# A two-layer diffusion trunk on one core: convolution gates by tanh, an earlier split of two gate slabs, lows on VectorE, and output projections in blocks of 512 columns

## The chip, the core and the metric

The kernel runs on one core of a Trainium2 chip. A core has a matrix engine (TensorE, in the profile PE, with its weight loads as PEld), a vector engine (VectorE, DVE), an engine for activation functions (ScalarE, ACT), a general engine (GpSimd, POOL) and SyncE (SP), whose queue starts all transfers that are spoken of here. Each engine works its instructions off in the order in which the program gave them; an instruction that has to wait holds up all behind it on its engine. SBUF is the memory on the chip, PSUM the banks that TensorE writes its products to, DRAM the memory beside it.

The metric is the time in microseconds (us) of one execution on the device. One execution is also recorded by the profiler; that record is the trace, and its summary is the page.

## The reference

Two layers, each with a token-mixing half and a channel half, on 512 latent tokens and 256 context tokens of width 1024, all in float32. The last layer gives the latent tokens alone, so that it needs only keys and values of the context. Cut to what matters here:

```python
hx = modulate(rmsnorm(x, norm1_g[i]), sx1, ax1)
px = hx @ w_in[i]          # conv input a, g | q | k | v | merge gates
z = a * jax.nn.sigmoid(g)                              # the convolution's gate
z = depthwise_conv(z, w_dw, width=31) + b_dw
y_conv = silu(layernorm(z)) @ w_conv_out
p = jax.nn.softmax(s, axis=-1)                         # 8 heads, two maps per head
w = p[:, :, 0] - lam * p[:, :, 1]
out = rmsnorm(w @ v, sub_g) * (1.0 - lam_init)
y_attn = out @ w_attn_out
g = jax.nn.sigmoid(gate_logits + b_gate)               # the merge gates, 2 x 1024 wide
x = x + gx1 * ((g_conv * y_conv + g_attn * y_attn) @ w_out)
x = x + gx2 * (square(relu(h2 @ w_mlp1)) @ w_mlp2)     # 4096 wide
```

The same runs on the context tokens with weights of the same name, in layer 0 whole, in layer 1 for keys and values.

## The kernel before, in words

**Products in three passes.** Every float32 operand x of a large product is split into a high part h (a copy in the matmul's own type, made on ScalarE) and a low part l = x - h (a subtraction). A product is three matmuls per contraction tile of 128, h by h, l by h and h by l (lines 142 to 144 in the trace). The splits are one helper; its high part is line 76 and its low part line 80, whichever tile they are for. Weights come in slabs of 1024 x 256, 1 MB each, into a staging tile (`r_...`), and are split there into `h_...` and `l_...`, each in two halves of 128x1024 elements. `load_slab` takes the engine of the lows: VectorE by default, GpSimd, or, with the pair `both`, one half on each.

**Stages of a layer.** (1) normalised input h1 in high and low, feature-major. (2) Attention, head by head: projections of q and k of the next head (`qk`, slabs `wqk`) and of v for the next pair of heads (`v`, slabs `wv`), scores `S`, exponentials `e` on ScalarE, the difference of the two maps on VectorE, transposes `wT` of the weights on TensorE, whose copies `wth`, `wtl` are made on ScalarE and VectorE, and the products `av`. (3) Convolution input `ca` and gate `cg`, two slabs each, four blocks of 128 features (`cg_0` to `cg_3`). (4) The merge gates `gt`, eight blocks for the attention branch (`gt_1_0` to `gt_1_7`, slabs `wg_1_0` to `wg_1_3`) and eight for the convolution (`gt_0_...`); meanwhile VectorE makes the convolution: 31 taps per block of channels, each tap one scalar_tensor_tensor into `crun` or, at the end, `cacc` (before: lines 1207 and 1211). (5) The branch projections `ya` and `yc`, the merged `mh`, `ml`. (6) The output projection `o` with residual and the sums of squares for the next norm. (7) The MLP (`f`, then `r`), in layer 0 by a scheme with fewer products, with a tail `r` that also ends in residual and sums of squares.

**What sets the order.** The function for a head is a generator; so are the projections and the conv blocks. `merge` draws from both in proportion to costs written in the code, head 7 with the conv blocks: `chain_(conv_a(0), conv_a(1), conv_g(0), conv_g1_ahead())`. A scheduler then orders each engine's instructions over the whole program, by its own estimates of when each can start; so an edit can move instructions far from the edited line. `issue_after` and `state["behind"]` name an instruction behind which others are put.

**Places that the change touches.** `conv_g`: four gate blocks go into PSUM tiles of two banks (`mm_tile`), ScalarE writes a sigmoid into a scratch tile with the tag `e0`, which the exponentials use too, and VectorE multiplies it into z. `conv_g1_ahead` takes one block of the second gate slab and then loads and splits the first merge-gate slab (1,0); slab (1,1) is split behind `ended`, the last head's final output copy. `spill_rstd`: the eight heads' reciprocal norms are transposed by TensorE (`rsT`), copied by VectorE (`rst`) and written to DRAM (`rs_d`). `branch_load` reads a head's output (`at_d` to `ar`) and, broadcast over the partitions, its reciprocal norm (`arb`), and VectorE multiplies them (before: line 1239). `out_slabs` makes the output projection (`o`) and the tail of the MLP (`r`); with a norm behind it, its first two slabs go by `halves`, that is column blocks of 256 tokens. `ada_beside` lays a count of small steps for the next layer's modulation beside each block.

## Time and profile before

| | |
|---|---|
| median of 3 runs | 2299.61 us (2297.89 to 2300.05) |
| profiled execution | 2294.07 us, span 2292.3 us |
| mean granted clock of TensorE | 0.995 |
| busy: PE, DVE, ACT, POOL | 97%, 73%, 46%, 29% |

The span is the time from the first to the last instruction; the rest of the execution's time lies around it. A row of waits reads: engine, its tile and line, "<-" the engine, tile and line that it waited for, then us in total, times, longest. A row in order of time reads: start, duration, engine, line, operation, tile written "<-" tiles read, shape; in brackets the idle time before it and what ended that. Matmuls are pipelined, so the distance of two starts, and not the duration, is what one costs.

Layer 0's conv gates lie at about 436 to 480 us of the span; layer 1's at about 1710 to 1742, its merge gates up to 1830, where `ya` begins.

### The profile page before, as it was taken

The numbers are of one execution on the slowest core, as the hardware profiler recorded it, in microseconds if no ns is written. First come the engines' busy times: TensorE is split into PE (matmuls) and PEld (weight loads), VectorE is DVE, ScalarE is ACT, GpSimd is POOL, SyncE is SP. The second block draws the span as 40 slices with busy tenths as digits, with TensorE's granted clock in tenths as the row PEclk, the third lists the DMA queues.
The fourth block names the chain that finished last, engine by engine and source line by source line (L and its number), as shares of the span: only waits on it lengthen the run. The fifth ranks groups of instructions, "written<-read, shape, count | busy, mean of one in ns | idle before, by whom it ended". The sixth has DMA issues, their size and how long they took to land.

```text
span 2292.3 us, 36448 instructions
## 1 busy us (share of the span) xinstructions
PE 2225.7 (97%) x14402; PEld 2015.7 (88%) x14402; DVE 1666.7 (73%) x2747; ACT 1053.5 (46%) x2049; POOL 655.3 (29%) x786
## 2 busy tenths in 40 slices
PE   7999999999999999999999998999999999999999
PEld 6999998888888999998999998999977889888887
DVE  6777776499657768787777567777758976757673
ACT  5555655422324264433445345565543333654542
POOL 1966775110000020222221347675722300100000
PEclk9999999999999999999999999999999999999999
DMA  9211111134444611332444522102114423443151
GB/s 318 60 34 44 47 46 47 45 116 160 138 150 147 212 46 57 98 119 88 132 139 142 167 75 58 45 24 63 45 61 130 131 93 120 147 129 100 66 184 37
DMA packets 202266, 232.62 MB, mean 101 GB/s; under 512 B 8864, under 2 KB 162928, under 8 KB 201968
## 3 DMA queue, kind: packets, MB, share of 16 engines
q1 hardware_dynamic: 202096, 230.30, 31.3%
q8 instruction: 113, 1.85, 0.3%
q14 instruction: 57, 0.47, 0.1%
HBM read 212.93 MB, written 17.35 MB: 100 GB/s over the span
## 4 chain that ended last, share of the span: by engine, by line
PE 73%; DVE 11%; ACT 5%; POOL 4%; DMA 4%; issue 2%; SPq 0%; DVEq 0%; POOLq 0%; ACTq 0%
PE r L151 4%; PE f L143 3%; PE f L144 3%; PE f L142 3%; PE r L143 3%; PE r L142 3%; PE r L144 3%; PE qk L142 2%; PE qk L143 2%; PE qk L144 2%; DVE crun L1211 2%; PE gt L142 2%; PE r L154 2%; PE gt L143 2%; PE gt L144 2%
## 5 line engine op out<-in xcount | busy, mean ns | idle before, releaser
L142 PE MATMUL qk<-h_wqk,h1h 128*128 128x256 f32 x640 | 182.6, 288 | 2.1 <-ACT rw L797 1.4
L143 PE MATMUL qk<-l_wqk,h1h 128*128 128x256 f32 x640 | 180.2, 284 | 0.0
L144 PE MATMUL qk<-h_wqk,h1l 128*128 128x256 f32 x640 | 176.4, 284 | 0.0
L969 DVE TENSOR_REDUCE st<-S 128x1 f32<-128x768 f32 (+1 forms) x160 | 134.5, 846 | 57.2 <-PE S L967 56.0
L972 ACT ACTIVATE e<-S,st 128x768 f32<-128x768 f32 (+1 forms) x160 | 131.0, 822 | 40.1 <-DVE st L969 39.8
L143 PE MATMUL f<-h2hl,h_w 128*128 128x512 f32 (+1 forms) x416 | 144.0, 348 | 1.1 <-POOL h2hl L80 0.9
L142 PE MATMUL f<-h2hh,h_w 128*128 128x512 f32 (+1 forms) x416 | 142.4, 348 | 2.1 <-ACT h2hh L387 1.1
L144 PE MATMUL f<-h2hh,l_w 128*128 128x512 f32 (+1 forms) x416 | 143.4, 346 | 0.0
L142 PE MATMUL gt<-h1h,h_wg 128*128 128x512 f32 (+1 forms) x384 | 137.5, 358 | 0.0
L143 PE MATMUL gt<-h1l,h_wg 128*128 128x512 f32 (+1 forms) x384 | 136.0, 354 | 0.0
L144 PE MATMUL gt<-h1h,l_wg 128*128 128x512 f32 (+1 forms) x384 | 135.9, 354 | 0.0
L151 PE MATMUL r<-F,whir 128*128 128x512 f32 (+1 forms) x384 | 123.9, 338 | 2.1 <-ACT F L1690 1.9
L142 PEld LDWEIGHTS qk<-h_wqk,h1h 128*128 128x128 f32 x640 | 122.1, 191 | 4.3 <-ACT rw L797 1.6
L151 PE MATMUL r<-F,wlor 128*128 128x512 f32 (+1 forms) x384 | 124.1, 339 | 0.5 <-POOL wlor L1608 0.3
L143 PEld LDWEIGHTS qk<-l_wqk,h1h 128*128 128x128 f32 x640 | 122.2, 191 | 0.3 <-POOL l_wqk L80 0.3
L1211 DVE SCALAR_TENSOR_TENSOR cacc<-z,cols,cacc 128x783 f32<-128x783 f32 x120 | 121.0, 1058 | 0.2
L144 PEld LDWEIGHTS qk<-h_wqk,h1l 128*128 128x128 f32 x640 | 119.9, 191 | 0.3 <-POOL h1l L80 0.2
L142 PE MATMUL v<-h_wv,h1h 128*128 128x256 f32 x384 | 112.1, 292 | 6.5 <-ACT rwc L861 3.2
L324 DVE SCALAR_TENSOR_TENSOR adaac<-ar,cvec,adaac 128x512 f32<-128x512 f32 x105 | 94.1, 916 | 31.6 <-DMA ar<-in_w_ada_dram 30.5
L144 PE MATMUL v<-h_wv,h1l 128*128 128x256 f32 x384 | 109.9, 286 | 0.0
L143 PE MATMUL v<-l_wv,h1h 128*128 128x256 f32 x384 | 109.4, 285 | 0.0
L803 POOL TENSOR_TENSOR rqk<-rqk,mhalf 128x4 f32<-128x4 f32 x80 | 85.9, 1077 | 78.6 <-DVE rqk L802 76.8
(406 smaller groups left out, 7539.8 us busy)
## 6 DMA issues: line engine op xcount, KB each, us to landing
r_w<-in_w_mlp_dram SPq DMA_DIRECT2D x34, 1024.0 KB, 5.4
ada<-in_w_ada_dram SPq DMA_DIRECT2D x24, 1024.0 KB, 5.5
ar<-in_w_ada_dram SPq DMA_DIRECT2D x96, 256.0 KB, 3.1
r_wg<-in_w_in_dram SPq DMA_DIRECT2D x16, 1024.0 KB, 5.2
r_wqk<-in_w_in_dram SPq DMA_DIRECT2D x30, 512.0 KB, 5.2
rf<-in_w_mlp_dram SPq DMA_DIRECT2D x26, 512.0 KB, 3.8
rr<-in_w_mlp_dram SPq DMA_DIRECT2D x24, 512.0 KB, 3.7
r_wao<-in_w_attn_out_dram SPq DMA_DIRECT2D x8, 1024.0 KB, 5.2
```

The costliest lines, as they stand in the source:

```text
L142: nc.tensor.matmul(ps, sh, mh, start=first, stop=False)
L143: nc.tensor.matmul(ps, sh, ml, start=False, stop=False)
L144: nc.tensor.matmul(ps, sl, mh, start=False, stop=last)
L151: nc.tensor.matmul(ps, w[j][:, k, m0 : m0 + P], a(k)[0][:, toks], start=k + j == 0, stop=False)
L154: nc.tensor.matmul(ps, w[0][:, k, m0 : m0 + P], a(k)[1][:, toks], start=False, stop=k == nk - 1)
L324: nc.vector.scalar_tensor_tensor(out=a, in0=r, scalar=cvec[:, k, q : q + 1], in1=a, op0=ALU.mult, op1=ALU.add)
L803: nc.gpsimd.tensor_tensor(out=r, in0=r, in1=mhalf[:, :4], op=ALU.pow)
L969: nc.vector.tensor_reduce(out=st[:, m : m + 1], in_=S[:, :nkey], axis=AX.X, op=ALU.max, negate=True)
L972: nc.scalar.activation(out=e[:, :nkey], in_=S[:, :nkey], func=AF.Exp, bias=st[:, m : m + 1], accum_out=st[:, 2 + m : 3 + m])
L1211: nc.vector.scalar_tensor_tensor(out=(run if t < TAPS - 1 else ca[cc])[:, :CV], in0=zt[cc][:, t : t + CV], scalar=wcol, in1=run[:, :CV], o ...
```

## The change

1. The convolution's gate: a is copied out of PSUM with the factor 0.5, ScalarE takes tanh(0.5 g) rather than sigmoid(g), and VectorE computes (tanh + 1) * z in one scalar_tensor_tensor. The scratch tile has the tags of two other tiles of the attention (three and four buffers) rather than `e0`.
2. Merge-gate slab (1,0) is split right behind the last gate block of conv slab 0, slab (1,1) behind the last gate block of conv slab 1.
3. In layer 1 the lows of the slabs for q, k and v are made on VectorE, both halves.
4. `spill_rstd` goes behind the sigmoid of merge-gate block (1,2).
5. The blocks of merge-gate slab (1,1) are put into four other PSUM banks (`mi`).
6. The output blocks of the first two slabs go by `groups`, 512 latent tokens and 256 context tokens, rather than by halves of 256. The counts for the modulation beside them are spread over the smaller number of blocks; their sums stay.

```diff
--- before.py
+++ after.py
@@ -728,7 +728,8 @@
                     ps = mm_tile(f"ca{i}_{cc}_{g.start}")
                     fm_block(ps[:, :W], w, m * P, lambda k: (hh[:, k], hl[:, k]), g)
                     z0 = PAD if g is LAT else ZC
-                    nc.scalar.activation(out=z[:, z0 : z0 + W], in_=ps[:, :W], func=AF.Copy)
+                    nc.scalar.activation(out=z[:, z0 : z0 + W], in_=ps[:, :W], func=AF.Copy,
+                                         scale=0.5)
                     if m == 0 and g is LAT:
                         conv_w[CONV_NEXT["a", s]] = conv_load(*CONV_NEXT["a", s])
                     yield 5.3 if g is LAT else 2.7
@@ -742,11 +743,13 @@
                     ps = mm_tile(f"cg{i}_{cc}_{g.start}")
                     fm_block(ps[:, :W], w, m * P, lambda k: (hh[:, k], hl[:, k]), g)
                     z0 = PAD if g is LAT else ZC
-                    sgt = ap.tile([P, 768], F32, tag="e0", name=f"sg{i}_{cc}_{g.start}", bufs=2)
-                    gated[:] = [nc.scalar.activation(out=sgt[:, :W], in_=ps[:, :W],
-                                                     func=AF.Sigmoid).ins]
                     zz = zt[cc][:, z0 : z0 + W]
-                    nc.vector.tensor_tensor(out=zz, in0=zz, in1=sgt[:, :W], op=ALU.mult)
+                    tag, n = ("dup", 3) if g is LAT else ("rw", 4)
+                    th = ap.tile([P, W], F32, tag=tag, name=f"th{i}_{cc}_{g.start}", bufs=n)
+                    gated[:] = [nc.scalar.activation(out=th, in_=ps[:, :W], func=AF.Tanh,
+                                                     scale=0.5).ins]
+                    nc.vector.scalar_tensor_tensor(out=zz, in0=th, scalar=1.0, in1=zz,
+                                                   op0=ALU.add, op1=ALU.mult)
                     if m == 0 and g is LAT and s == 0:
                         conv_w["g", 1] = conv_load("g", 1)
                     yield 5.3 if g is LAT else 2.7
@@ -760,12 +763,10 @@
 
         def conv_g1_ahead():
 
-            g = conv_g(1)
-            yield next(g)
             state["behind"] = tuple(gated)
             gate_slab(1, 0, nc.gpsimd)
             state["behind"] = ()
-            yield from g
+            yield from conv_g(1)
 
 
         sqs = [ap.tile([P, 4, QK + 1], F32, tag=f"sqe{n}", name=f"sqe{i}_{n}", bufs=1) for n in range(2)]
@@ -780,7 +781,7 @@
 
             pre = first.pop("ps") if h == 0 else []
             state["behind"] = turned.pop(h - 1, ())
-            w = first.pop("w") if h == 0 else qk_slab(i, h, both)
+            w = first.pop("w") if h == 0 else qk_slab(i, h, None if last else both)
             state["behind"] = ()
             QA = qp.tile([P, 4 * NT + 2 * nv], F32R, tag="qk", name=f"qk{i}_{h}")
             QH = QA[:, : 4 * NT].rearrange("p (g d) -> p g d", g=4)
@@ -920,7 +921,7 @@
                 yield 0.5
 
         def v_pair(pr):
-            w = first.pop("v") if pr == 0 and "v" in first else v_slab(i, pr, both)
+            w = first.pop("v") if pr == 0 and "v" in first else v_slab(i, pr, None if last else both)
             vh, vl = (ap.tile([P, NTT, 256], F32R, tag=tg, name=f"{tg}{i}_{pr}")
                       for tg in ("vh", "vl"))
             for j in range(2):
@@ -1163,7 +1164,7 @@
             if h == H - 1:
                 main = chain_(main, rest_of(carry))
             merge(main, chain_(*fill), fc / att_cost)
-        state["behind"] = tuple(ended)
+        state["behind"] = tuple(gated)
         gate_slab(1, 1)
         state["behind"] = ()
         for pl in (psx, pspool, apool):
@@ -1262,7 +1263,8 @@
                 if (half, s) not in wg:
                     gate_slab(half, s, nc.gpsimd if last else None)
                 if (half, s) == (1, 2):
-                    drain(spill_rstd())
+                    with tc.issue_after(opened):
+                        drain(spill_rstd())
                 if half == 0 and s == 3 and not last:
                     for hg in branch[:4]:
                         branch_load(*hg)
@@ -1283,11 +1285,14 @@
                     lst[mb] = t
                     for g in groups:
                         W = g.stop - g.start
-                        ps = ps_for(g, f"gt{i}_{half}_{mb}_{g.start}")
+                        ps = (state["mi"] if (half, s) == (1, 1) else lambda name: ps_for(g, name))(
+                            f"gt{i}_{half}_{mb}_{g.start}")
                         fm_block(ps[:, :W], w, m * P, lambda k: (hh[:, k], hl[:, k]), g)
                         bcol = R_BG + half * KT + mb
-                        nc.scalar.activation(out=t[:, g], in_=ps[:, :W], func=AF.Sigmoid,
-                                             bias=cols[:, bcol : bcol + 1])
+                        sg_ = nc.scalar.activation(out=t[:, g], in_=ps[:, :W], func=AF.Sigmoid,
+                                                   bias=cols[:, bcol : bcol + 1]).ins
+                        if (half, mb, g.start) == (1, 2, 0):
+                            opened = sg_
                     some_taps(per_gate)
                     if m == 0 and not state.get("ada_done"):
                         ada_slab(i, L, 8 + 4 * half + s)
@@ -1453,7 +1458,7 @@
 
             for s in range(2 if norm else 4):
                 w = load(s)
-                for g in halves if norm else groups:
+                for g in groups:
                     for m in range(2):
                         out_block(w, s, g, m, hidden, gate, nm, norm)
                         if tick:
@@ -1511,7 +1516,7 @@
         out_slabs(lambda s: load_slab(rows(w_out[i], 256 * s, 256), f"wo{i}_{s}"),
                   lambda k: (mh[k], ml[k]), gate1, f"o{i}", norm2, None,
                   (lambda: mlp1_slab(0, 0), second_ahead),
-                  None if last else ada_beside(*[1] * 10, 2, 2, 2, 2, 1))
+                  None if last else ada_beside(2, 2, 1, 1, 2, 2, 2, 2, 2, 2, 1))
 
 
         accp.__exit__(None, None, None)
@@ -1977,7 +1982,7 @@
                     w_mlp2[i][3072:4096, 256 * s : 256 * s + 256]
                     .rearrange("(k p) n -> p k n", p=P), f"w2_{i}_{s}", lo_eng=nc.gpsimd),
                 lambda k: tuple((F if k < HK else F7)[:, j, k % HK] for j in range(2)),
-                gate2, f"r{i}", norm1, after, tick=ada_beside(2, 2, 2, 2, *[1] * 8), ahead=
+                gate2, f"r{i}", norm1, after, tick=ada_beside(3, 3, 2, 2, 2, 2, 1, 1), ahead=
                 (lambda: first.update(w=qk_slab(i + 1, 0, nc.gpsimd)), v_first))
             state["ada_done"] = True
             ada_gain(Ln, 1, ns=1)
```

How instructions move, at three places. First ScalarE at the end of layer 0's attention (`sg` the sigmoid, `th` the tanh, `e` an exponential, `g` a merge gate). Before:

```order
L76 ACTIVATE wth_7_1_1_5567<-wT_7_3_1_5773 128x3x128
L746 ACT_TABLE_LOAD
L746 ACTIVATE sg_0_0_5851<-cg_0_0_5826 128x512
L746 ACTIVATE sg_0_512_5911<-cg_0_512_5886 128x256
L972 ACT_TABLE_LOAD
L972 ACTIVATE e_7_5_5924,st_7_5_5919<-S_7_5_0_5920,st_7_5_5919 128x256
L1010 ACTIVATE osq_7_1_5881<-av_7_1_5862 128x256
...
L746 ACT_TABLE_LOAD
L746 ACTIVATE sg_1_0_5962<-cg_1_0_5937 128x512
```

and after:

```order
L749 ACTIVATE th_1_0_5962<-cg_1_0_5937 128x512
...
L973 ACTIVATE e_7_5_5930,st_7_5_5919<-S_7_5_1_5926,st_7_5_5919 128x256
L749 ACTIVATE th_1_512_6012<-cg_1_512_5987 128x256
...
L749 ACTIVATE th_2_0_6048<-cg_2_0_6023 128x512
L749 ACTIVATE th_2_512_6081<-cg_2_512_6056 128x256
L1011 ACTIVATE osq_7_1_5881<-av_7_1_5862 128x256
...
L1026 ACTIVATE rsall_711<-av_7_2_5975,es_7_2_5781 128x1 x2
L1292 ACT_TABLE_LOAD
L1292 ACTIVATE g_1_0_6161<-gt_1_0_0_6162,cols_115 128x512
```

The loads of ScalarE's table between exponential and gate are gone, the gate blocks stand nearer to their matmuls, and one load stands ahead of the first merge gate.

Second, TensorE at the end of layer 1's attention (`wT_7_3` the last transposes, `av_7_1` the last product, `osq` its squares, `rsT` the reciprocal norms). Before:

```order
L144 MATMUL cg_3_0_19013<-h1h_13563,l_wcg_1_18903 128x512
L995 MATMUL wT_7_3_1_18914<-cst,e_7_3_18845 128x128 x3
...
L143 MATMUL gt_1_0_0_19063<-h1l_13564,h_wg_1_0_19007 128x512
L144 MATMUL gt_1_0_0_19063<-h1h_13563,l_wg_1_0_19008 128x512
...
L142 MATMUL av_7_1_18920<-wth_7_1_1_18724,vh_3_17428 128x256
L144 MATMUL gt_1_0_0_19063<-h1h_13563,l_wg_1_0_19008 128x512
...
L1021 MATMUL av_7_1_18920<-cst,osq_7_1_18939 128x1 x2
L144 MATMUL gt_1_1_0_19098<-h1h_13563,l_wg_1_0_19008 128x512
...
L1058 MATMUL rsT_19207<-cst,rsall_14618 32x128
L142 MATMUL gt_1_2_0_19132<-h1h_13563,h_wg_1_1_19043 128x512
```

and after:

```order
L144 MATMUL gt_1_1_0_18870<-h1h_13449,l_wg_1_0_18752 128x512
L996 MATMUL wT_7_3_0_18680<-cst,e_7_3_18617 128x128 x3
L142 MATMUL av_7_1_18692<-wth_7_1_0_18494,vh_3_17200 128x256
L996 MATMUL wT_7_3_1_18686<-cst,e_7_3_18617 128x128 x3
...
L143 MATMUL av_7_1_18692<-wtl_7_1_1_18497,vh_3_17200 128x256
L144 MATMUL av_7_1_18692<-wth_7_1_1_18496,vl_3_17201 128x256
L1022 MATMUL av_7_1_18692<-cst,osq_7_1_18711 128x1 x2
L142 MATMUL gt_1_2_0_18904<-h1h_13449,h_wg_1_1_18815 128x512
...
L144 MATMUL gt_1_3_0_18938<-h1h_13449,l_wg_1_1_18816 128x512
L1059 MATMUL rsT_18979<-cst,rsall_14390 32x128
L142 MATMUL gt_1_4_0_18985<-h1h_13449,h_wg_1_2_18973 128x512
```

Conv gate blocks 2 and 3 and both blocks of merge-gate slab (1,0) come ahead of the last transposes, and the transpose of the reciprocal norms stands behind blocks 2 and 3 of the merge gates.

Third, VectorE around the copy of the reciprocal norms in layer 1 (`crun` are taps of the convolution). Before:

```order
L80 TENSOR_TENSOR wtl_7_1_1_18725<-wT_7_3_1_18914,wth_7_1_1_18724 128x3x128
L1211 SCALAR_TENSOR_TENSOR crun_0_19089<-z_18576,cols_8470,crun_0_19089 128x512
...
L1211 SCALAR_TENSOR_TENSOR crun_0_19089<-z_18576,cols_8470,crun_0_19089 128x512
L1060 COPY rst_19209<-rsT_19207 32x128
L1211 SCALAR_TENSOR_TENSOR crun_1_19242<-z_18576,cols_8470,crun_1_19242 128x512
...
L1211 SCALAR_TENSOR_TENSOR crun_1_19242<-z_18576,cols_8470,crun_1_19242 128x512
L1239 TENSOR_TENSOR ar_0_0_19365<-ar_0_0_19365,arb_0_0_19367 128x512
L1211 SCALAR_TENSOR_TENSOR crun_0_19089<-z_18576,cols_8470,crun_0_19089 128x512
L1239 TENSOR_TENSOR ar_1_0_19372<-ar_1_0_19372,arb_1_0_19374 128x512
```

and after:

```order
L80 TENSOR_TENSOR wtl_7_1_1_18497<-wT_7_3_1_18686,wth_7_1_1_18496 128x3x128
L1212 SCALAR_TENSOR_TENSOR crun_0_18861<-z_18348,cols_8470,crun_0_18861 128x512
...
L1212 SCALAR_TENSOR_TENSOR crun_1_19014<-z_18348,cols_8470,crun_1_19014 128x512
L1061 COPY rst_18981<-rsT_18979 32x128
L1212 SCALAR_TENSOR_TENSOR crun_0_18861<-z_18348,cols_8470,crun_0_18861 128x512
...
L1212 SCALAR_TENSOR_TENSOR crun_1_19014<-z_18348,cols_8470,crun_1_19014 128x512
L1240 TENSOR_TENSOR ar_0_0_19137<-ar_0_0_19137,arb_0_0_19139 128x512
L1212 SCALAR_TENSOR_TENSOR crun_0_18861<-z_18348,cols_8470,crun_0_18861 128x512
L1240 TENSOR_TENSOR ar_1_0_19144<-ar_1_0_19144,arb_1_0_19146 128x512
```

Between the last `wtl` and the copy there are 22 taps (before, among other rows, 16), between the copy and the first product 8 (before 15).

## The prediction

> **What bounds the kernel now.** I read the page first, then the waits of TensorE, then the stretches where it stood still, by windows and in order of time.
>
> The page's first two lines:
>
> ```profile
> span 2292.3 us, 36448 instructions
> PE 2225.7 (97%) x14402; PEld 2015.7 (88%) x14402; DVE 1666.7 (73%) x2747; ACT 1053.5 (46%) x2049; POOL 655.3 (29%) x786
> ```
>
> TensorE (PE) is busy for 97% of the span. An edit can therefore win in three ways only: matmul time, the 67 us in which PE is idle, or time at a reduced clock. The waits of PE over the whole span, of which I keep the rows that the change touches:
>
> ```profile
> PE wT L995 <- DVE wtl L80: 5.1, 9, 0.9
> PE qkT L835 <- POOL dup L821: 4.0, 5, 1.3
> PE cg L142 <- ACT sg L746: 3.9, 2, 2.5
> PE v L142 <- DVE vl L80: 2.6, 6, 0.6
> PE ya L142 <- DVE cacc L1211: 0.7, 1, 0.7
> ```
>
> The third is the conv gate: its matmuls (cg) wait for a bank which the sigmoid (sg) has not read yet. Windows of layer 0's and layer 1's ends of attention, and of layer 1's gate stage and attention (us, then busy time of PE, PEld, DVE, ACT, POOL, then the granted clock):
>
> ```profile
> 440.00:460.00 20.00, 16.76 (x104) 14.48 (x104) 9.96 (x22) 8.69 (x21) 2.69 (x7) 1.00 0.18 60
> 1715.00:1730.00 15.00, 11.52 (x57) 9.34 (x56) 7.23 (x13) 6.38 (x13) 1.13 (x3) 0.89 0.03 9
> 1800.00:1840.00 40.00, 39.33 (x173) 32.12 (x172) 40.00 (x59) 12.14 (x17) 8.12 (x4) 1.00 0.24 80
> 1380.00:1720.00 340.00, 322.06 (x2375) 302.15 (x2373) 240.28 (x402) 188.10 (x415) 202.13 (x278) 0.98 0.17 50
> ```
>
> PE loses 3.2 us at the first place and 3.5 us at the second, where the clock also falls. In layer 1's gate stage VectorE (DVE) is the full engine, and PE only just keeps busy.
>
> **Term 1, blocks of 512.** Two matmuls of 256 columns become one of 512. First and last start of a run of 43 steps, and of one of 35 steps:
>
> ```profile
> 746.78 0.28 PE L143 MATMUL o<-ml,h_wo 128*128 128x256 f32 x1
> 751.93 0.28 PE L144 MATMUL o<-mh,l_wo 128*128 128x256 f32 x1
> 1765.00 0.39 PE L143 MATMUL gt<-h1l,h_wg 128*128 128x512 f32 x1
> 1772.93 0.39 PE L142 MATMUL gt<-h1h,h_wg 128*128 128x512 f32 x1
> ```
>
> Steps are 5.15/43 = 0.120 us and 7.93/35 = 0.227 us, so a pair saves 2 x 0.120 - 0.227 = 0.013 us. The code has 3 calls x 2 slabs x 2 blocks x 8 contraction tiles x 3 products = 288 pairs: **3.7 us**. Rounding the starts allows 2.8 to 3.9. DVE's residuals and ScalarE's squares merge with them and get fewer, off the path.
>
> The Trainium skill, "TensorE: Matmul & The Clock Gate", section "Back-to-back issue gap", gives an isolated gap of N/2.4 + 2.5 ns: 109 ns at 256 columns and 216 at 512. By it a pair saves 2.5 ns and the edit 0.7 us. The rows here show 120 and 227, so I go by the rows; the rule is rival C.
>
> **Term 2, tanh at layer 0's end of attention.** ScalarE (ACT) there:
>
> ```profile
> 453.25 1.28 ACT L746 ACT_TABLE_LOAD   x1
> 454.54 0.60 ACT L746 ACTIVATE sg<-cg 128x512 f32<-128x512 f32 x1
> 456.30 1.28 ACT L972 ACT_TABLE_LOAD   x1
> 457.60 0.48 ACT L972 ACTIVATE e<-S,st 128x256 f32<-128x256 f32 x1
> 461.57 1.28 ACT L746 ACT_TABLE_LOAD   x1
> ```
>
> Sigmoid and exponential alternate and each pays 1.28 us. Built with tanh, the program holds no load between exponential and gate; one remains per layer, ahead of the first merge gate's sigmoid, where the bank is not urgent. Besides, the gate's scratch no longer shares buffers with the exponentials, so the sigmoid need not follow them. Of the 3.2 us lost in the window I take **2.5**; the other 0.7 is waiting for wth and wtl copies that stay. Bounds: 0 (another wait takes the place) to 3.2.
>
> By the same skill, "ScalarE: Activation LUTs", section "What ACT_TABLE_LOAD costs", a load brings a drain of about 1380 ns too. Here the load ending at 454.53 is followed by an ACTIVATE at 454.54, so the trace shows none, and the 1.28 stands.
>
> **Term 3, layer 1's end of attention and gate stage.** The chain before, ACT, then PE, then DVE:
>
> ```profile
> 1723.94 0.49 ACT L76 ACTIVATE wth<-wT 128x384 fp32r<-128x384 f32 x1 [0.44 <-PE wT L995]
> 1724.45 1.28 ACT L746 ACT_TABLE_LOAD   x1
> 1725.74 0.60 ACT L746 ACTIVATE sg<-cg 128x512 f32<-128x512 f32 x1
> 1726.39 0.68 PE L142 MATMUL cg<-h1h,h_wcg 128*128 128x512 f32 x1 [2.49 <-ACT sg L746]
> 1726.86 0.63 PE L143 MATMUL cg<-h1l,h_wcg 128*128 128x512 f32 x1
> ```
>
> PE stands 2.5 us until the first sigmoid has freed a bank, then steps at 0.43 to 0.47 us, half pace. The window's 3.5 us and its clock (0.11 x 15 = 1.7 us) make 5.2 us lost. The order after drains the conv gates and both blocks of the first gate slab ahead of the last transposes, so that work no longer lies among them as filler, and the short copies behind them show. Their durations:
>
> ```profile
> 1724.46 0.56 DVE L80 TENSOR_TENSOR wtl<-wT,wth 128x384 fp32r<-128x384 f32 x1 [1.16 <-ACT wth L76]
> 1726.37 0.69 DVE L749 TENSOR_TENSOR z<-z,sg 128x512 f32<-128x512 f32 x1 [1.35 <-ACT sg L746]
> 1746.85 0.38 ACT L1010 ACTIVATE osq<-av 128x256 f32<-128x256 f32 x1 [5.27 <-PE av L144]
> ```
>
> One pair of wth and wtl (0.49 + 0.56) and the squares (0.38) are 1.4 us, two pairs with a reader that comes too early 3. So PE comes to gate block 2 between 2.2 and 3.8 us earlier, less if the clock falls again.
>
> What is late next is DVE. Its taps fill the stage (40.00 of 40), and the rows around the attention's rstd are:
>
> ```profile
> 1754.06 0.28 DVE L1060 COPY rst<-rsT 32x128 f32<-32x128 f32 x1 [0.47 <-PE rsT L1058]
> 1754.26 9.95 DVE L1211 SCALAR_TENSOR_TENSOR crun<-z,cols,crun 128x512 f32<-128x512 f32 x15
> 1766.38 2.45 DVE L1239 TENSOR_TENSOR ar<-ar,arb 128x512 f32<-128x512 f32 x1 [2.16 <-DMA arb<-rs_d]
> 1833.60 0.73 PE L142 MATMUL ya<-h1h,h_wao 128*128 128x512 f32 x2 [0.67 <-DVE cacc L1211]
> ```
>
> From the copy to the first product it takes 12.1 us (the write and the broadcast read through DRAM): 15 taps of 0.66 us and 2.2 us of standing. After, the transpose of rstd goes behind gate block 3, and only 8 taps (5.3 us) lie between copy and product, so DVE may stand up to 12.1 - 5.3 = 6.8 us. Queued behind the product on DVE are the other taps and the splits that ya reads, and PE waits for these. DVE begins the taps sooner by the load (1.28) and by what the gate's matmuls come sooner, some 3 us; its end lies between 3 us earlier (standing as before) and 3 - 4.6 = 1.6 us later. With the 0.7 us that ya waits now, the stage hands on between 3.7 us sooner and 1.6 later. I take **2**, the upper half, since the taps that have left the place between copy and product have run ahead and are not lost.
>
> The smaller edits of this stage get nothing: z by scalar_tensor_tensor is a tap's 0.66 us in place of 0.69; no wait row names a bank of the merge gates (gt), so other banks remove none. The load of gate slab (1,1) moves ahead of head 7's first output on SP:
>
> ```profile
> 1722.35 0.32 SPq L1014 DMA_DIRECT2D at_d<-uo  x1
> 1752.73 2.36 SPq L1234 DMA_DIRECT2D ar<-at_d  x3
> ```
>
> That output is read again 30 us on, which hides it; without this cover the output would be late by what the load waits for its buffer, some 10 us before the rstd product, and count as rival A.
>
> **Term 4, lows on DVE in layer 1.** Ten slabs have one half low (the low parts of a weight) on DVE and one on GpSimd (POOL). All uses by the tile's summary, and one pair in order of time:
>
> ```profile
> L80 POOL TENSOR_TENSOR l_wqk<-r_wqk,h_wqk x18: 2355/2408/3381, 17.3 to 1625.3; 128x1024 fp32r<-128x1024 f32 x18
> L80 DVE TENSOR_TENSOR l_wqk<-r_wqk,h_wqk x14: 1212/1397/3248, 60.9 to 1626.4; 128x1024 fp32r<-128x1024 f32 x14
> 1459.74 2.40 POOL L80 TENSOR_TENSOR l_wqk<-r_wqk,h_wqk 128x1024 fp32r<-128x1024 f32 x1 [0.86 <-ACT h_wqk L76]
> 1459.97 3.25 DVE L80 TENSOR_TENSOR l_wqk<-r_wqk,h_wqk 128x1024 fp32r<-128x1024 f32 x1
> ```
>
> Beside POOL's half DVE's takes 3.25 us, alone 1.21 (the minimum): two alone are 2.42. So POOL loses 24 us of work and DVE's price per slab goes from between 1.2 and 3.3 to 2.4, level in the sum. What it can win are waits behind the pair: 2.6 us (v for vl) and part of the 4.0 (qkT for dup). What it can lose is 1.2 us per slab where the pair did not collide. I take **1**, bounds 3 and -3 (rival B goes further).
>
> **Sum.** 3.7 + 2.5 + 2 + 1 = 9.2 us. The profiled execution took 2294.07, so its like would take 2284.9. The runs shown have a median of 2299.61, 5.5 above the profiled one; against it the forecast is **2290.4**. All terms at their good end make 3.9 + 3.2 + 3.7 + 3 = 13.8 (2285.8), at their bad end 2.8 + 0 - 1.6 - 3 = -1.8 (2301.4).
>
> **The rivals.** A measurement tells about 0.2% here, 4.6 us: faster is under 2295.0, slower above 2304.2.
>
> A, layer 1's gain is handed back at ya. For it: DVE at 40.00 of 40, and the wait on arb already there. Against: DVE starts sooner. Term 3 becomes -1.6 to 0: 2299.6 - (3.7 + 2.5 + 1) and 0 to 1.6 more = 2292.4 to 2294.0.
>
> B, DVE becomes the engine that attention in layer 1 waits for. It is busy 240.28 of 340 us, and PE already waits for its wtl and vl. A second low stands in DVE's queue ahead of them: at worst 10 x 1.21 = 12.1 us, and from an average of 0.8 us a slab on it eats all other gains (8.2). At the full price: 2299.6 + 12.1 - 8.2 = 2303.5, and above 2304.2 if term 3 fails too (2305.5). It decides if the row of PE waiting for wtl, now 5.1, goes above 12. Against it: DVE has 100 us free there, and POOL's work no longer stretches its lows.
>
> C, matmuls gain by the isolated gap: 0.7 instead of 3.7, 2293.4.
>
> D, the waits merely move: the standing for banks turns into standing for wth, wtl and rstd, and the change of clock stays. Then terms 2 to 4 are nothing and the spacing alone is left: 2295.9, no change that a measurement shows.
>
> **How the numbers follow.** Forecast (all terms near what I take) 0.5; A 0.18; C 0.05; D 0.17; B 0.08; the rest 0.02 lies below 2285. Faster: 0.47 of the forecast's, A's 0.15, 0.03 of C, 0.07 of D, 0.02 of the rest: 0.74. Slower: 0.06, most of B. Same: 0.20. The range takes in A, C, D and the good end, and leaves out most of B: 2284 to 2299.
>
> **What would show it.** In the profile after: no ACT_TABLE_LOAD among the exponentials, "cg <- sg" gone and no like row "cg <- th"; o and r with 288 matmuls of 512 columns more at 0.227 us steps; l_wqk on DVE at 1.21 us, in pairs; waits for wtl not over 6; DVE standing for arb between 2 and 7 us, and the row of ya waiting for DVE not over 3. I am wrong if the layer 1 attention (1380 to 1720) is no shorter or the wait at ya grows by as much as its end came sooner.

## The result, and the profile after

The changed kernel takes 2284.69 us (median of 4 runs, 2283.22 to 2285.89) against 2299.83 us (median of 4 runs) of the kernel before: a ratio of 0.9938, interval 0.992 to 0.9957. A second comparison, on another chip, gave 2283.59 against 2297.81 and 0.9934 (0.9919 to 0.995). The forecast was 2290.4: faster, but by 9.2 us where it is 14 to 15.

The page after, its first two lines:

```profile
span 2284.1 us, 35819 instructions
PE 2225.1 (97%) x14114; PEld 2004.8 (88%) x14114; DVE 1658.1 (73%) x2736; ACT 1047.6 (46%) x2035; POOL 642.9 (28%) x776
```

The 288 matmuls fewer are there (14402 to 14114). The waits of TensorE after, those that answer to the rows shown of before:

```profile
PE wT L996 <- DVE wtl L80: 3.8, 6, 0.9
PE qkT L836 <- POOL dup L822: 3.3, 3, 1.3
PE ya L142 <- ACT h1h L76: 3.0, 1, 3.0
PE ya L142 <- DVE cacc L1212: 0.8, 1, 0.8
PE v L142 <- DVE vl L80: 0.2, 1, 0.2
```

The row "cg <- sg" (3.9 us) is gone and no "cg <- th" came; "v <- vl" fell from 2.6 to 0.2, wtl from 5.1 to 3.8. One row has grown: ya for the split h1h of an attention output, 1.7 before. The windows that the prediction showed, after (the last is from another place in the work, since the stages come earlier):

```profile
440.00:460.00 20.00, 20.00 (x126) 17.96 (x125) 10.03 (x22) 7.29 (x20) 1.54 (x5) 1.00 0.19 60
1380.00:1720.00 340.00, 327.78 (x2428) 309.63 (x2427) 239.60 (x418) 192.00 (x421) 185.32 (x277) 0.98 0.16 50
1715.00:1730.00 15.00, 15.00 (x82) 12.89 (x81) 13.56 (x21) 6.71 (x14) 5.84 (x5) 1.00 0.25 81
```

In these windows TensorE no longer stands at either end of attention, and in layer 1's attention it is busy for 327.78 us of 340 where it was 322.06. ScalarE's table loads went from ten to eight: the five at lines 746 and 972 became one at line 973 and these two, at 492.0 and 1746.2 us, each ahead of the first merge gate:

```profile
L1292 ACT ACT_TABLE_LOAD x2 | 2.6, 1283 | 0.0
```

Where the time went is best seen by stages. The table gives, from the first and last start of each tile's matmuls in each trace, the length of a stage in us. "A0 end" is from layer 0's first cg to its first gt, "G0" from there to its first yc, "o0" from the first o to the first f, "mlp0" from the first f to layer 1's first kc, "A1" from there to layer 1's last score, "E1" from there to its last yc, "o1" from there to the last o.

```
kernel                        A0 end    G0    o0    mlp0     A1     E1    o1
before                          47.0  225.2  70.3  557.1  338.6  186.7  47.0
after                           43.2  229.1  68.8  561.3  329.6  185.3  46.0
after, second trace             43.2  228.8  68.8  559.0  329.0  185.1  46.0
lows alone (e1)                 47.0  225.4  70.1  556.3  330.5  187.1  47.0
blocks alone (e2)               47.0  227.3  68.8  556.0  335.8  192.5  46.0
tanh alone (e3)                 41.8  226.5  70.6  558.2  337.3  187.0  47.0
tanh, slabs, spill, banks (e4)  43.2  226.1  70.1  561.0  338.1  189.4  47.0
after without the lows (e5)     43.2  226.3  68.8  560.1  336.5  186.3  46.0
lows on GpSimd (e7)             47.0  227.5  70.4  558.1  332.6  191.3  47.0
```

"After, second trace" is e13, the changed kernel once more. The gain of the whole change lies in layer 1's attention (9 us) and in the three projections (1.4 and 1.0 us at o; the third lies in mlp0, where the tail r of layer 0 takes 69.45 us from first to last start for 70.69). Layer 0's end of attention is 3.8 us shorter, and in these two traces the gate stage behind it is as much longer.

**The clock.** One plain thing has to be known to read such differences. In every one of the 14 traces some stretches run at half clock (granted clock 0.50): 3.4, 6.8 or 10.2 us long but for one that the end of the program cuts off, each behind idle time of TensorE that adds up to 1.2 to 4.0 us in the 7 us ahead of it, and not all at the same places in two executions of one kernel. A stretch costs half of its length. Each run's mean granted clock is on record; time x mean clock takes this cost out. For one kernel this product is known to within 0.5 to 1.2 us (standard error over its runs), so a difference of two by itself to within about 0.7 to 1.7. The mean clock of the kernel before is 0.9929 and 0.9932 on two chips, for the changed kernel 0.9942. The profiled execution of before (0.995) was a lucky one, which is why its span of 2292.3 lies so far under the median.

Two more things about the table. A1 and E1 meet at layer 1's last score, which an edit can move among the gate blocks, so their sum is the safer figure. Without the cost of the half-clock stretches in them, A1 and E1 together are 518.4 us before, 509.8 and 510.7 in the changed kernel's two traces, 510.7 in e1, 518.0 in e2, 517.5 in e3, 520.7 in e4, 517.7 in e5 and 517.0 in e7: by this, what is gained in layer 1 is gained by the lows.

### The profile page after: what moved, and what is told of

Read it like the earlier page. It is cut to its first block, busy times and chain, and to the rows that moved or that the text cites. A ratio compares the mean times of both kernels' runs of the same rounds, so it can differ in the third digit from the quotient of the medians.

```text
span 2284.1 us, 35819 instructions
## 1 busy us (share of the span) xinstructions
PE 2225.1 (97%) x14114; PEld 2004.8 (88%) x14114; DVE 1658.1 (73%) x2736; ACT 1047.6 (46%) x2035; POOL 642.9 (28%) x776
## 4 chain that ended last, share of the span: by engine, by line
PE 75%; DVE 11%; ACT 4%; DMA 4%; POOL 3%; issue 2%; SPq 0%; DVEq 0%; POOLq 0%; ACTq 0%
PE r L151 5%; PE f L143 3%; PE f L144 3%; PE f L142 3%; PE r L142 3%; PE r L144 3%; PE r L143 3%; DVE crun L1212 3%; PE r L154 2%; PE qk L142 2%; PE qk L143 2%; PE qk L144 2%; PE gt L142 2%; PE gt L143 2%; PE gt L144 2%
```

## The experiments

In one table: the ratio to the kernel before on the same chip, the means of time and clock, and time x clock (in brackets that of the kernel before beside it; e1 to e4 shared a chip, so did e13, e5, e8 and e12, and e6, e7, e9 and e14).

```
kernel                          ratio (interval)         mean us  clock   time x clock
e1 lows alone                   0.9976 (0.9966, 0.9986)  2290.2   0.9934  2275.0 (2281.5)
e2 blocks alone                 1.0010 (1.0001, 1.0019)  2298.8   0.9918  2280.0 (2281.5)
e3 tanh alone                   0.9993 (0.9980, 1.0005)  2296.0   0.9928  2279.5 (2281.5)
e4 tanh, slabs, spill, banks    0.9997 (0.9984, 1.0009)  2296.3   0.9936  2281.6 (2281.5)
e13 the changed kernel          0.9934 (0.9919, 0.9950)  2282.9   0.9942  2269.6 (2282.2)
e5 changed, lows as before      0.9982 (0.9973, 0.9990)  2293.6   0.9929  2277.4 (2282.2)
e8 changed, lows in layer 0 too 0.9958 (0.9945, 0.9972)  2289.0   0.9952  2278.0 (2282.2)
e12 changed, blocks as before   0.9960 (0.9945, 0.9976)  2288.8   0.9937  2274.3 (2282.2)
e6 changed, spill as before     0.9952 (0.9940, 0.9963)  2285.1   0.9930  2269.1 (2280.7)
e7 lows on GpSimd alone         1.0000 (0.9988, 1.0012)  2296.5   0.9930  2280.5 (2280.7)
e9 changed, slabs as before     0.9995 (0.9986, 1.0003)  2294.8   0.9912  2274.6 (2280.7)
e14 changed, one load later     0.9939 (0.9928, 0.9951)  2282.3   0.9944  2269.5 (2280.7)
```

### The lows: e1, e5, e7, e8

e1, the kernel before with edit 3 alone:

```diff
-            w = first.pop("w") if h == 0 else qk_slab(i, h, both)
+            w = first.pop("w") if h == 0 else qk_slab(i, h, None if last else both)
```

and the same for `v_slab`.

> The kernel before with edit 3 alone: in layer 1 both halves of the lows of ten slabs on VectorE. Theory P (the prediction's term 4): 1 us faster, 3 faster to 3 slower. Theory Q, formed from the two traces, in which layer 1's attention from its first score to the last projection (about 1380 to 1700 us) came out 8 us shorter with all edits together: the pair of halves that ran at the same time on VectorE and GpSimd held up the copies queued behind it, and 6 to 9 us of the gain come from this edit alone. Q also expects the waits for vl (2.6 us before) and part of those for wtl and dup gone, and POOL busy 24 us less. Rival B (VectorE becomes the bound) expects it slower by up to 12 us.

Measured: 2290.2 us in the mean against 2297.8, 6.5 us by time x clock; layer 1's attention (A1) is 8.1 us shorter, 1.7 of it one half-clock stretch less. Theory Q holds, the prediction's 1 us does not. Layer 1's weights alone, by the tile's summary over 1376 to 1712 us, before:

```profile
L80 DVE TENSOR_TENSOR l_wqk<-r_wqk,h_wqk x7: 1212/2425/3248, 1384.9 to 1626.4; 128x1024 fp32r<-128x1024 f32 x7
L80 POOL TENSOR_TENSOR l_wqk<-r_wqk,h_wqk x7: 2381/2402/2496, 1385.9 to 1625.3; 128x1024 fp32r<-128x1024 f32 x7
```

and in e1:

```profile
L80 DVE TENSOR_TENSOR l_wqk<-r_wqk,h_wqk x14: 1217/1220/1226, 1387.6 to 1623.6; 128x1024 fp32r<-128x1024 f32 x14
```

The median on VectorE goes from 2.4 to 1.2 us, with nothing on GpSimd. That alone is level, as the prediction had it. What it left out is the work around it. Groups by form on VectorE between 1400 and 1690 us, before (busy us, mean ns of one):

```profile
L982 DVE SCALAR_TENSOR_TENSOR e<-e,st,e 128x768 f32<-128x768 f32 x29 | 31.5, 1086 | 0.8
L80 DVE TENSOR_TENSOR wtl<-wT,wth 128x384 fp32r<-128x384 f32 x55 | 30.4, 553 | 13.9 <-ACT wth L76 13.3
L821 DVE TENSOR_TENSOR dup<-ra,rb 128x256 f32<-128x256 f32 x27 | 17.0, 628 | 10.2 <-POOL rb L816 10.2
```

in e1:

```profile
L982 DVE SCALAR_TENSOR_TENSOR e<-e,st,e 128x768 f32<-128x768 f32 x29 | 31.0, 1071 | 0.8
L80 DVE TENSOR_TENSOR wtl<-wT,wth 128x384 fp32r<-128x384 f32 x56 | 31.0, 553 | 18.5 <-ACT wth L76 17.9
L821 DVE TENSOR_TENSOR dup<-ra,rb 128x256 f32<-128x256 f32 x28 | 13.2, 472 | 4.0 <-POOL rb L816 3.9
```

`dup` gets 0.16 us cheaper and waits 6 us less for GpSimd's `rb`, which stood behind the lows there. TensorE's listed waits in 1376 to 1712 add up to 18.0 us before and 13.8 in e1. The rows that changed most, before:

```profile
PE v L142 <- ACT rwc L861: 3.2, 3, 1.2
PE v L142 <- DVE vl L80: 2.4, 5, 0.6
PE v L142 <- DVE qk L842: 0.7, 1, 0.7
```

and in e1, where "v <- vl" is none:

```profile
PE v L142 <- ACT rwc L861: 0.6, 1, 0.6
PE v L142 <- DVE qk L842: 3.5, 2, 2.8
```

Waits (4.2 us) and clock (1.7) make 5.9 of the 8.1 us; the rest stands in no wait row.

e7, the control: the same lows all on GpSimd.

```diff
-            w = first.pop("w") if h == 0 else qk_slab(i, h, both)
+            w = first.pop("w") if h == 0 else qk_slab(i, h, nc.gpsimd if last else both)
```

> The kernel before with both halves of layer 1's ten lows on GpSimd, none on VectorE. If the cost before was the collision of the two halves (VectorE's half stretched from 1.2 to 3.3 us, with its copies queued behind it), this is faster than before too, by up to the 6 to 8 us of e1. If instead it is GpSimd's own work that TensorE waits for (the rows qkT for dup), with 24 us more on GpSimd it is slower than before, by 5 us or more, and the waits for dup and h_wqk's low grow from 4 us to over 8.

Measured: ratio 1.0000; neither of the two. A1 is 6.0 us shorter and E1 4.6 us longer, so that 1.4 us are left in this trace, with or without the clock, and nothing in the mean. The pair's collision is gone, but GpSimd's halves now collide with other work of VectorE. The same groups in e7:

```profile
L982 DVE SCALAR_TENSOR_TENSOR e<-e,st,e 128x768 f32<-128x768 f32 x29 | 39.4, 1359 | 0.7
L80 DVE TENSOR_TENSOR wtl<-wT,wth 128x384 fp32r<-128x384 f32 x56 | 30.9, 553 | 15.5 <-ACT wth L76 15.0
L821 DVE TENSOR_TENSOR dup<-ra,rb 128x256 f32<-128x256 f32 x28 | 21.2, 757 | 15.0 <-POOL rb L816 14.9
```

`e` goes from 1071 to 1359 ns and `dup` from 472 to 757, while wtl stays at 553 in all three. The first two read two operands from SBUF; wtl reads one from SBUF and one (wT) from PSUM. Taken one by one it is plainer: the 8 of the 29 `e` that a low on GpSimd overlaps take 1941 ns in the mean, the other 21 take 1137; 6 of the 28 `dup` take 1533 against 546; 8 of the 56 wtl that a low overlaps for over a fifth of their time take 556 against 552. Two lows of GpSimd, one behind the other, with a wtl and then an `e` of VectorE beside them, in order of time:

```profile
1461.70 4.96 POOL L80 TENSOR_TENSOR l_wqk<-r_wqk,h_wqk 128x1024 fp32r<-128x1024 f32 x2 [0.31 <-ACT h_wqk L76]
1463.71 0.56 DVE L80 TENSOR_TENSOR wtl<-wT,wth 128x384 fp32r<-128x384 f32 x1
1465.84 1.64 DVE L982 SCALAR_TENSOR_TENSOR e<-e,st,e 128x768 f32<-128x768 f32 x1
```

So a low on GpSimd is paid for a second time on VectorE, in work with two operands from SBUF that runs beside it. The Trainium skill says this in "SBUF — State Buffer", section "Who interferes with whom": a VectorE instruction with two SBUF inputs contends with a GpSimd instruction that reads SBUF, one with at most one such input doesn't, outside VectorE's 2-port modes. The three groups agree with it. That this collision is all that keeps e7 from gaining is not shown: most of the time comes back in E1, behind the last of these lows.

e8, the changed kernel with layer 0's lows on VectorE too:

```diff
-            w = first.pop("w") if h == 0 else qk_slab(i, h, None if last else both)
+            w = first.pop("w") if h == 0 else qk_slab(i, h)
```

> The changed kernel with the lows for q, k and v on VectorE in layer 0 too. If the collision of the two halves is what costs, layer 0's ten pairs are worth about as much as layer 1's, 0.6 to 0.8 us each: 5 to 8 us faster than the changed kernel. If it was the load on GpSimd that mattered: layer 0's VectorE and GpSimd are busy for 261 and 217 of 360 us, about as in layer 1 (240 and 202 of 340), so the same. If layer 0's 768 query rows make VectorE the bound there: slower by up to 12 us.

Measured: 0.9958, about 6 us slower than the changed kernel beside it (2289.0 against 2282.9), 8.4 by time x clock, and layer 0's attention, from first score to first ca, takes 310.9 us where it took 304.5. So in layer 0 the third expectation has the sign right. That VectorE is the bound there is not shown: it is busy for 240.5 of the 310.9 us, for 235.3 of the 304.5 in the changed kernel. Why the move gains nothing is in the same rows. Layer 0's lows between 84 and 390 us in the changed kernel:

```profile
L80 DVE TENSOR_TENSOR l_wqk<-r_wqk,h_wqk x6: 1211/1264/1773, 106.0 to 334.0; 128x1024 fp32r<-128x1024 f32 x6
L80 POOL TENSOR_TENSOR l_wqk<-r_wqk,h_wqk x6: 2391/2504/3378, 108.5 to 337.2; 128x1024 fp32r<-128x1024 f32 x6
```

There VectorE's half starts first in all eight pairs of the stretch (106.0 against 108.5 at the first), and it takes 1.26 us in the median and not 2.4; where the two overlap, it is GpSimd's half that is stretched, to 3.38 us. In layer 1 before, GpSimd's half starts first in eight of the ten pairs (the one that the prediction shows: 1459.74 against 1459.97), and in seven of these eight VectorE's takes 2.4 to 3.4 us. So in layer 0 there is hardly a stretch of VectorE's to remove, and a move mostly adds a second half to VectorE. Same edit, opposite sign, told by one number, the duration of VectorE's half.

e5, the changed kernel with edit 3 undone:

> The changed kernel with the lows of layer 1 back on VectorE and GpSimd, a half each (edit 3 undone). Theory Q: 6.5 to 9 us slower than the changed kernel, as in e1, since the gain lies in the ten pairs in layer 1's attention. Theory P (the prediction's term): 1 us slower. Theory I: over 9 us slower, since the rest then falls back to what e4 and e2 showed, about the time of the kernel before.

Measured: 2293.6 against 2282.9 us, 10.7 us slower, 7.8 by time x clock. A1 is 336.5 against 329.0 to 329.6. That is Q; what goes beyond 9 us lies in the clock.

### The blocks: e2, e12

e2, the kernel before with edit 6 alone:

```diff
-                for g in halves if norm else groups:
+                for g in groups:
```

with the counts for the modulation as in the change.

> The kernel before with edit 6 alone: output blocks of 512 and 256 columns instead of three of 256. By the distance of matmul starts (0.120 and 0.227 us) 288 pairs save 3.7 us, 2.8 to 3.9; by the isolated gap 0.7 us. If the merged blocks make the squares and the norm behind them later than before, the gain is smaller than 3.7 and the rest is seen at the norm's start.

Measured: 1.0010, no gain. Yet the stages gain what was worked out: o0 70.3 to 68.8, o1 47.0 to 46.0, mlp0 557.1 to 556.0, together 3.6 us. In this trace it comes back as clock. The scheduler puts layer 1's heads 6 and 7 in another order, far from any edited line; A1 and E1 together are 3.1 us longer, and the half-clock stretches in them cost 3.4 us more than before. A like stretch in layer 0's gate stage (G0), where the order is as before, costs 1.7 more. Windows of 10 us around layer 1's wait for sg, before and, in the second block, in e2 (the first pair of numbers is TensorE's, the granted clock stands behind GpSimd's):

```profile
1720.00:1730.00 10.00, 6.52 (x29) 5.02 (x29) 6.27 (x11) 5.07 (x11) 1.13 (x3) 0.83 0.04 13
1730.00:1740.00 10.00, 10.00 (x53) 8.39 (x52) 10.00 (x16) 3.48 (x5) 4.26 (x2) 1.00 0.00 1
```

```profile
1720.00:1730.00 10.00, 8.33 (x50) 6.95 (x48) 2.64 (x5) 3.66 (x10) 1.12 (x3) 1.00 0.16 55
1730.00:1740.00 10.00, 8.30 (x26) 6.60 (x27) 7.90 (x13) 2.72 (x4) 0.00 (x0) 0.66 0.01 2
```

The same 2.5 us wait for sg costs (1 - 0.83) x 10 = 1.7 us of clock before and 3.4 us in e2. Over all runs e2's mean clock is 0.9918 against 0.9929, 2.5 us. By time x clock e2 is 1.5 us faster (standard error 0.7); where the other 2 us went stays open.

e12, the changed kernel with edit 6 undone:

> The changed kernel with the output blocks by halves of 256 again (edit 6 undone). By the matmul starts it is 3.7 us slower than the changed kernel. By e2, where the edit alone gave no gain, with 1.2 us less at each of the three projections and the rest lost where its new order of layer 1's last head collides: 0 to 3.7 us slower, and the projections by themselves 1.2 us longer each.

Measured: 2288.8 against 2282.9 us, 4.7 us slower by time x clock. With the wait for the gate gone, the 3.7 us stay won, within the spread of the runs. E12 also has TensorE wait 2.7 us at "ln <- DVE tot" (0.6 in the changed kernel), so not all of the 4.7 us need be the blocks' own.

### The ends of attention: e3, e4, e9, e6

e3, the kernel before with edit 1 alone (tanh, the factor 0.5, the scratch tags).

> The kernel before with edit 1 alone: tanh instead of sigmoid in the convolution's gate, with the other scratch tags. The prediction's terms 2 and 3 together gave 4.5 us for the edits 1, 2, 4 and 5. In the two traces layer 0's end of attention gained 3.8 us, which were gone again at the end of ya, and layer 1's 4.3 us, of which 2 went at ya. If the tables alone do it, this edit gives all that the four give: 2 to 3 us faster, with layer 0's end of attention 3 to 4 us shorter and ya waiting longer for the split behind it. If the early slabs are needed, it gives under 1 us.

Measured: 0.9993 (0.998 to 1.0005), no difference by time; 2.1 us faster by time x clock, with a standard error of 0.8. Layer 0's end of attention is 5.2 us shorter (A0 end 41.8), with tanh alone. In layer 1 a wait took the place of the one removed, and the clock fell behind it. Waits of TensorE in 1690 to 1770 us of e3, first row, and its windows:

```profile
PE rsT L1061 <- POOL rsall L1031: 2.9, 1, 2.9
```

```profile
1740.00:1750.00 10.00, 7.02 (x43) 5.95 (x41) 9.99 (x16) 4.26 (x9) 0.27 (x1) 0.99 0.04 13
1750.00:1760.00 10.00, 8.69 (x27) 6.73 (x28) 10.00 (x16) 4.58 (x6) 2.27 (x2) 0.67 0.69 224
```

TensorE arrives at the transpose of the reciprocal norms before the last of them is made, stands 2.9 us, and loses 3.3 us more of clock.

e4, the edits 1, 2, 4 and 5:

> The kernel before with edits 1, 2, 4 and 5: tanh, the earlier split of two merge-gate slabs, the later spill of the reciprocal norms, the other banks; lows and output blocks as before. The prediction: 4.5 us faster (terms 2 and 3). From the traces: 2 to 4 us, since layer 0's 3.8 us are handed back at ya. With e1 and e2 it should add up to the whole change (15 us against the median): if Q holds, 7 + 3.7 + 4 = 15.

Measured: 0.9997, no gain by time x clock. E1 is 2.8 us longer than before, with TensorE waiting 2.7 us for the convolution's sum and the clock at 0.80 and 0.86 in the two windows of 10 us from 1830 on:

```profile
PE ln L1316 <- DVE tot L1313: 2.7, 1, 2.7
```

That is near the prediction's rival A (the gain handed back behind VectorE at the end of the gate stage), in the kernel without the other edits; in the changed kernel the same row is 0.6 us.

e9, the changed kernel with edit 2 undone, the slabs split at the old places:

> The changed kernel with the two merge-gate slabs split at the old places (edit 2 undone). If tanh alone shortens the end of layer 0's attention (e3: from 47.0 to 41.8 us, with the early slabs 43.2), it is the same as the changed kernel or up to 1.5 us faster there; in layer 1 the split of slab (1,1) behind the last head's output lets merge-gate block 2 wait for its low: 1 to 4 us slower.

Measured: 0.9995. Against the changed kernel's like on that chip (e14) it is 12.5 us slower, 5.1 by time x clock and the rest clock (0.9912, the lowest of all): by time far more than the 4 us expected at most. And it is not by the row that was expected: merge-gate blocks wait 0.3 us for a low of their slab. Two other waits stand out, in layer 0 and layer 1 (0.8 and 0.7 us in the kernel before):

```profile
PE adaps L260 <- DMA ada<-in_w_ada_dram: 4.9, 1, 4.9
PE ya L142 <- DVE cacc L1214: 3.7, 1, 3.7
```

The first is at about 500 us: the old place lets the loads of slab (1,1) (476.2 us against 465.8) and of the modulation weights (499.5 against 489.2) go later on SyncE, and TensorE meets a load that is not there. E3, also tanh without the early slabs, has this load as late (498.6) and no such wait: its order has the matmuls that need it at 505.1, not at 500. So the early slabs are needed in the changed kernel's order, and not by tanh as such.

e6, the changed kernel with the spill at its old place:

> The changed kernel with the spill of the reciprocal norms at its old place (edit 4 undone). With tanh alone (e3) TensorE stood 2.9 us at the transpose rsT for the last head's rsall and then ran some 3.3 us at half clock. Theory W (the move of the spill takes that wait away and is needed once the conv gate is early): the row 'rsT <- POOL rsall' is back with about 3 us, and the kernel is 2 to 5 us slower than the changed one. The prediction's rival A (the later spill makes VectorE stand for arb and ya wait): this kernel is as fast or up to 2 us faster, since VectorE's wait for arb falls from 3.1 to under 1 us.

Measured: 0.9952 (0.994 to 0.9963), 2285.1 us; by time x clock level with the changed kernel's like on that chip (e14, 2269.1 and 2269.5). The wait "rsT <- rsall" isn't among its rows and E1 is 185.2, as with the edit. Theory W is not borne out in this order, nor is rival A's gain: VectorE stands 2.9 us for arb here and 3.1 with the edit. Whether edit 4 is worth anything stays open: by time the kernel without it is 2.8 us slower (2285.1 against 2282.3), by time x clock nothing of this is left.

### A load of layer 0: e14

```diff
-                ada_slab(i, L, 16 + s)
+                with tc.issue_after(state["ar"].ins):
+                    ada_slab(i, L, 16 + s)
```

where `state["ar"]` is the last load of an attention output.

> The changed kernel with one load of layer 0's modulation weights (1 MB) put behind the last load of a head's output (ar) on SyncE. In layer 0 the attention's end came out 3.8 us earlier and ya's end not at all: ya waits 3.0 us for h1h, whose ar was issued at 634.3 us and landed at 644.2, behind two loads of 1 MB. If these loads hand the gain back: the wait falls under 1 us and the kernel is 2 to 4 us faster than the changed one, faster than both kernels. If the buffer or another load is what the ar waits for: the same.

Measured: 0.9939 (0.9928 to 0.9951), the same as the changed kernel on the other chips. The row "ya <- h1h" is gone as expected, and another stands in its place, again the late load that gave way:

```profile
PE adaps L260 <- DMA ada<-in_w_ada_dram: 2.3, 1, 2.3
```

Both loads are wanted in one stretch, so the wait only moves. SyncE in the changed kernel, in order of time (start, duration):

```profile
630.55 0.80 SPq L105 DMA_DIRECT2D ada<-in_w_ada_dram  x1
633.11 0.44 SPq L124 DMA_DIRECT2D r_wao<-in_w_attn_out_dram  x1
634.32 3.19 SPq L1235 DMA_DIRECT2D ar<-at_d  x1
```

VectorE takes up that ar at 644.18, 9.9 us after its issue behind 2 MB. The wait that this edit aims at is 0.9 to 1.7 us in e4, e5, e6 and e12, which have the changed kernel's order there, so there was less to win than the first trace showed. None of the versions beats the changed kernel.

e13 is the changed kernel once more:

> The changed kernel once more, on the same chip as the three beside it. The first comparison had four runs of each and gave 0.9938 (0.992 to 0.9957). Each edit alone (e1, e2 and e4, by their ratios) adds up to about 5.5 us, by their means to 8. Theory A (the edits add up): 0.996 to 0.9975. Theory I (they help each other in layer 1, whose attention and tail came out 11.2 us shorter in the whole change's trace against 6.9 and 2.5 for the lows and the tail alone): 0.993 to 0.9945.

Measured: 0.9934. That is Theory I's range. By the ratios e1, e2 and e4 alone add up to 0.17%, 3.9 us (5.5 is e1 by itself), the whole to 0.66%. By time x clock they add up to 8.0 us (6.5 + 1.5 + 0), the whole to 12.6; this difference of 4.6 has a standard error of about 2.3. So the edits help each other, and a good part of that is clock. It is not layer 1's attention and tail, as Theory I had it: without the clock's cost the whole gains 7.7 to 8.7 us there and e1 alone 7.7. Undone one at a time they are worth 7.8 (lows) and 4.7 (blocks).

## Why the prediction was right or wrong

**The bound and the side.** Right: TensorE bound before and after, and the three ways to win (matmul time, waits, clock) are the ones that moved. The time is 5.7 us under the forecast and inside the range.

**Term 1, 3.7 us.** Right in size and in how it is made: three projections give 1.4, 1.0 and 1.2 us. Two rows of o in the changed kernel:

```profile
748.84 0.39 PE L142 MATMUL o<-mh,h_wo 128*128 128x512 f32 x1
751.78 0.39 PE L143 MATMUL o<-ml,h_wo 128*128 128x512 f32 x1
```

13 steps of 0.226 us. Rival C, the isolated gap, falls: 0.7 us would not be seen in o0 and o1 at all. What the prediction lacked is that the edit alone gives nothing by time (e2), since it treated an edit's cost as lying where its lines are.

**Term 2, 2.5 us.** The mechanism was right, and A0 end gained more than was taken (3.8 us, 5.2 in e3). The gate stage behind it is longer: by 3.6 to 3.9 us in both traces of the changed kernel, 1.7 of it a half-clock stretch (clock 0.91 over the 20 us from 640), so that nothing is left there. But e4, e5, e6 and e12 have the same order of instructions as the changed kernel on TensorE, VectorE, ScalarE and GpSimd up to layer 0's output projection, and in them A0 end and G0 together take 268.7 to 269.4 us where the two traces of the changed kernel take 272.3 and 272.0. The kernels with the old order there (before, e1, e2, e7) take 272.1, 272.3, 274.3 and 274.5. In the mean that is 273.3 against 270.1, a gain of 3.2 us: the term was about right, and the two traces of the changed kernel were unlucky ones here. What differs between executions of one order is ya's wait for h1h, a transfer behind two others (1.7 before; 3.0 and 2.7 in the two traces, 0.9 to 1.7 in the other four), and the clock behind it. The prediction put no next wait behind this term, and this is the one. Rival A's handing back is seen in layer 0, where it was not placed, in some executions only. Whether the tables or the other scratch tags of edit 1 gain the time was not tried apart.

**Term 3, 2 us.** E1 is 1.4 to 1.6 us shorter: near in size, but by the clock alone. The trace before has a half-clock stretch behind the wait for sg (1726.5, 1.7 us of cost), the two traces of the changed kernel have none in E1; without it E1 is 185.0 us before and 185.3 and 185.1 after. TensorE's standing in E1 hardly changed (4.5 to 4.2 us): the wait for sg is gone, and small ones stand in its place (av for wtl 0.8 and for wth 0.6, ln for tot 0.6, and av for uo 0.9 where it was 0.5), as rival D had it. VectorE stands 3.12 us for arb where it stood 2.16 and up to 6.8 was allowed:

```profile
1757.28 0.27 DVE L1061 COPY rst<-rsT 32x128 f32<-32x128 f32 x1
1757.48 5.34 DVE L1212 SCALAR_TENSOR_TENSOR crun<-z,cols,crun 128x512 f32<-128x512 f32 x8
1765.95 0.69 DVE L1240 TENSOR_TENSOR ar<-ar,arb 128x512 f32<-128x512 f32 x1 [3.12 <-DMA arb<-rs_d]
```

From the copy to the product it is 8.5 us now, not 12.1, since the broadcast reads begin 4.9 us behind the write (1762.49 against 1757.58) where it was 7.0 (1762.16 against 1755.18). The 12.1 us were taken as a fixed length, which they are not; why the way through DRAM got shorter was not tried. The product itself takes 0.69 us, not 2.45: before, two lows of GpSimd began half a us ahead of it, the collision of term 4 in another place.

```profile
1765.88 5.22 POOL L80 TENSOR_TENSOR l_wg<-r_wg,h_wg 128x1024 fp32r<-128x1024 f32 x2 [3.01 <-ACT h_wg L76]
```

"The smaller edits get nothing" stays open for the spill (e6) and the banks, which were not tried alone, and is wrong for the early slabs: without them (e9) the term and more is lost.

**Term 4, 1 us.** This is the term that was mis-sized, 7 to 8 us against 1, above its bound of 3. "Level in the sum" holds for the pair itself: VectorE's half takes 2425 ns in the median in layer 1, two alone take 2440. (The 1397 ns that the prediction shows mix both layers.) The step that failed is what it counted as to be won, TensorE's two rows for vl and dup. It took VectorE's other work at a fixed length and GpSimd's 24 us as work that nobody waits for. The runs showed `dup` 0.16 us cheaper each, VectorE's wait for `rb` 6 us shorter, TensorE's "v <- rwc" 2.6 us shorter, and a half-clock stretch less. How the 7 to 8 us divide among these stays open. Rival B, VectorE as the bound, does not hold in layer 1. In layer 0, where it was not placed, the same edit costs 6.4 us (e8), with VectorE not full.

**The sum.** Without the clock's cost the stages of the changed kernel's two traces gain 3.7 (the projections), 1.6 and 1.9 (A0 end and G0), and 8.7 and 7.7 us (A1 and E1): 14.0 and 13.3, against 12.6 by time x clock over all runs and 14 to 15 by time; what lies between the last two is the clock (0.9942 against 0.9932, 2.3 us). The prediction took the clock only as part of term 3. Terms 1 and 2 came about as taken, and the miss of 5.7 us is term 4. That term 3 came near is in part luck, since of the standing and the clock that it counted only the clock went. Rival D (the waits merely move) is true of E1 and of the singles e3 and e4 there, and false of the whole.

## What to carry to other kernels

Price an operation on VectorE and GpSimd together: look at the duration of VectorE's half in the stage in question, not over the program, and if it is stretched, the pair collides and VectorE alone may do better (GpSimd alone did not, e7); where it isn't stretched, moving work over mostly adds to the busier one. When a stall goes, ask at once what load or result the engine will now meet too early, and move that forward with it: by time the changed kernel without the early slabs lost all that it had won (e9). Where a scheduler orders the program, an edit may pay or cost far from its lines, so read each stage's length and the granted clock before calling a total the edit's worth, and read them in more than one execution: one and the same order gained 3.4 us in one trace and nothing in another.

## What the runs showed of the hardware that was not expected

GpSimd's subtractions of 128x1024 (2.4 us each) lengthen VectorE's two-operand work beside them when both operands lie in SBUF: 472 ns without them, 628 with ten in the stage and 757 with twenty for one form, 1071, 1086 and 1359 for another, and not when one lies in PSUM (553 in all three). Of two like subtractions, the one that starts second is the one stretched most: in layer 1 before, VectorE's to 3.2 to 3.4 us where GpSimd's begins 0.1 to 0.2 us ahead; in layer 0, GpSimd's to 3.4 where VectorE's begins 0.4 to 0.7 us ahead and itself takes 1.5 and 1.8.

Waits of TensorE that add up to little over 1 us can cost more than themselves: every half-clock stretch in the 14 traces that ends before the program does has 1.2 to 4.0 us of idle time in the 7 us ahead of it, and each is 3.4, 6.8 or 10.2 us long. Behind the same 2.5 us wait the clock cost 1.7 us in one trace and 3.4 us in another. The Trainium skill, "TensorE: Matmul & The Clock Gate", section "Part 1: The HAM clock gate (the "warmup" mystery)", has a gate that looks at free-running windows of about 3.4 us; the losses here, 1.7 and 3.4 us, are one and two such windows at half clock. That its phase is what differs between executions is argued, not shown.
